# A transformer layer on one Trainium2 core: stores of the mixing part on SyncE's queue, w_o's sums on GpSimd behind markers, a second z, and GpSimd's arithmetic on VectorE

## The chip, the cores and the metric

The kernel runs on one core of one Trainium2 chip. The core has TensorE (PE in the profile; matmuls), VectorE (DVE), ScalarE (ACT), GpSimd (POOL) and SyncE (SP), which here does nothing but start DMA transfers. GpSimd starts DMAs as well: the two are the kernel's two DMA queues, and only GpSimd's can add to what is in DRAM. Each engine works off its own instructions in a fixed order; an instruction that waits holds up everything behind it on that engine, the start of a DMA too. The metric is the device time of one execution in microseconds (us); lower is better.

## The reference, cut to what matters

One layer over 512 tokens of width 2048, float32. The mixing part (attention with 8 heads of width 128, beside pooling) comes first, the feed-forward part after it:

```python
h = rms_norm(x, pre_mix_g)
z = h @ w_in                       # 2048 x 4096: [q | k | v | u], 1024 columns each
a = chunked_attention(q, k, v, rel_bias)   # 8 heads, chunks of 64 tokens
p = multiscale_pool(u, pool_w, pool_scale) # 4 groups, trailing means of 2, 4, 8, 16 tokens
x = x + rms_norm(concat(a, p) @ w_o, post_mix_g)
h = rms_norm(x, pre_ffn_g)
y = (gelu(dwconv3(h @ w_up)[:F]) * dwconv3(h @ w_up)[F:]) @ w_down
x = x + rms_norm(y, post_ffn_g)
```

In the pooling, a trailing mean is made from running sums (each doubling step adds a shifted copy), minus the token itself. In the attention, a mask puts −1e30 where a chunk would look ahead.

## The kernel before, in words

**Split products.** Each float32 operand is split into a rounded part and the rest: `split` (L136) has ScalarE write the rounded part (L138) and VectorE the rest (L139, or L142 with a scale). A product then takes three matmuls (`mm3`: L156, L158, L159), or a wide and a half one (`mm2`: L164, L170). A weight block is loaded by SP into a raw tile (`raw4`, five buffers), then split into `w4` tiles (names ending in h and l).

**Seven products for eight.** The large products are done by a scheme of seven block products, whose operands are sums of blocks of the weights and of x. Head 0's q and k are done plainly at the start, with x coming in. After that come the v stage for half of v (`v_steps(0)`), then the products for q and k of the other seven heads, pair by pair: `Pairs` loads four raw blocks ww, wx, wy, wz for each pair on SP (L444), `make` adds them on VectorE and splits each sum into wfh and wfl some four products ahead, `qk_product` does the matmuls and `qk_keep` gathers the seven results (za, zb, zm) into the tile z, 128 x 2 x 512, which holds q and −k of one head. There is one buffer for z. Each z is stored to DRAM, `zqk[h]`, by GpSimd (L567).

**The heads.** Then come heads 0 to 2, between the steps of the second half of v, and heads 3 to 7 between the eight blocks of u (`u0` to `u7`). `load_head` (L632) loads the head's bias and its zq on SP, multiplies zq by RR (the norm's factors) on GpSimd (L638), and splits it into qkh and qkl. `scores` does the score matmuls (s, L156 to L159) and the softmax on VectorE and ScalarE, with a memset of −1e30 on GpSimd for each of four blocks (L670); `turn` transposes the probabilities (pt, L688) and splits them into pth and ptl; `values` multiplies by v. The values of v wait in DRAM (`vd`, stored by `v_spill`, L393) and are loaded by `v_load` in two loads of 512 KB.

**Pooling.** `pool_keep` makes the running sums us from u with up to four additions on GpSimd (L710), and `pool_mix` multiplies by the group's matrix (pm). `spill_mix` writes the result to the single tile mx and stores it to `pooled` from GpSimd (L739).

**Work laid in between.** Two kinds of work prepare for later. *Ready blocks*: six parts of blocks of w_down are split early and stored as `rw..h` and `rw..l` (`keep_ready`, L275); `READY_AT` says at which v step. *Sums in DRAM*: `sums_in_dram` builds the sums of w_o's blocks (and of some of w_down's) in DRAM, wt and t, without the core's memory: a copy by SP (L306, not ahead of the last weight load), then additions by GpSimd (L309), step by step (`more_sums`). An addition waits for the copy under it.

A scheduler sets each engine's order from the code and from when tiles come free, and `issue_after` puts one instruction behind another, so the order shown below isn't the code's.

Of the kernel before, what the change touches and what calls it, by code (L numbers as in the profile page):

```python
# [9 lines left out]
F32 = mybir.dt.float32  # L10
F32R = mybir.dt.float32r
AF = mybir.ActivationFunctionType
ALU = mybir.AluOpType
# [32 lines left out]
def f32(ap):  # L46
    return ap.bitcast(F32)
# [32 lines left out]
def encoder_layer(ctx: ExitStack, tc: tile.TileContext, x, xT, vecs, rel, post_mix, post_ffn,  # L80
# [29 lines left out]
    def raw4(name):  # L110
        return big.tile([P, 1024], F32, tag="raw", bufs=5, name=name)
# [142 lines left out]
    READY = (0, 1), (1, 1), (0, 2)  # L254
    ready_w = {at: [dram.tile([P, CU, S], F32, name=f"rw{at[0]}{at[1]}{p}") for p in "hl"] for at in READY}

    READY_AT = {0: (7,), 1: (3, 4, 5, 6, 7)}
    ready_parts = [(at, j) for at in READY for j in range(2)]
    READY_OF = {0: ready_parts[:1], 1: ready_parts[1:]}

    def v_and_ready_specs(g):
        specs = []
# [7 lines left out]
    def keep_ready(g, n):  # L270
        if n not in READY_AT[g]:
            return
        (cc, i), j = READY_OF[g][READY_AT[g].index(n)]
        for dest, v in zip(ready_w[cc, i], weights.get(f"rw{cc}{i}_{j}")):
            nc.gpsimd.dma_start(dest[:, 2 * j:2 * j + 2, :], f32(v))  # L275

    specs = v_and_ready_specs(0)
    FIRST_PART = len(specs)
# [22 lines left out]

    def sums_in_dram():

        def copy(dest, source):
            with tc.issue_after(load_w.last):
                nc.sync.dma_start(dest, source)  # L306

        def add(dest, source):
            nc.gpsimd.dma_start(dest, source, accum_op=ALU.add)  # L309

        def wo_step(step, i, at):
            for cc in range(2):
                source = wo_block(cc, *at) if type(at) is tuple else wo_sum[at][cc]
                for k in range(2):
                    sl = slice(4 * k, 4 * k + 4)
                    step(wo_sum[i][cc][:, sl, :], source[:, sl, :])
                    yield

        for step, i, at in ((copy, 7, (1, 1)), (add, 7, (0, 1)), (copy, 5, (0, 0)), (add, 5, (0, 1)),
                            (copy, 6, 5), (add, 6, (1, 1)), (copy, 4, 6), (add, 4, (1, 0))):  # L320
            yield from wo_step(step, i, at)
# [46 lines left out]
    z0 = raw4("z0").rearrange("p (a b) -> p a b", a=2)  # L368
    nc.scalar.activation(z0[:, 0], ps0["q"], AF.Copy)
    nc.vector.tensor_scalar_mul(z0[:, 1], ps0["k"], -1.0)  # L370
    nc.gpsimd.dma_start(zqk[0], z0)

    def v_steps(i, ps):
        for n, c in enumerate(VORDER[i]):
# [13 lines left out]
    def v_spill(i, ps):  # L388
        for p in range(2):
            v = raw4(f"vs{p}").rearrange("p (a b) -> p a b", a=2)  # L390
            for t in range(2):
                nc.scalar.activation(v[:, t], ps[2 * p + t], AF.Copy)
            nc.gpsimd.dma_start(vd[i][:, 2 * p:2 * p + 2, :], v)  # L393

    def scaled(q):
        for kb in range(4 * q, 4 * q + 4):
# [32 lines left out]
    class Pairs:  # L429
# [12 lines left out]
        def load(self, k, i):  # L442
            def raw(what, tile_, m, kh):
                load_w.last = nc.sync.dma_start(tile_, w_qk[k + 1, m, kh]).ins  # L444
                self.raw[k, what] = tile_

            if i == 1:
                raw("x", p0.tile([P, 1024], F32, tag="wx", bufs=3, name="wx"), 0, 0)
                raw("w", raw4("ww"), 1, 0)
            elif i == 2:  # L450
                raw("z", p0.tile([P, 1024], F32, tag="wz", bufs=2, name="wz"), 0, 1)
            elif i == 5:
                raw("y", raw4("wy"), 1, 1)

# [58 lines left out]
    def more_sums(n):  # L513
        for _ in range(n):
            next(sums_step, None)

    BANK = {1: "a", 6: "a", 7: "a", 4: "a", 5: "g", 3: "g", 2: "d"}
    FIRST = 1, 5, 2
    TURNED = 6, 7, 4
# [21 lines left out]
    def qk_keep(k, i):  # L541
        if i == 1:
            qk_z[k, "1"] = qk_tile("za", 1, 2)
            nc.scalar.activation(whole_of(qk_z[k, "1"]), qk_banks[k, "a"], AF.Copy)
        elif i == 2:
            v = whole_of(qk_z[k, "1"])
            nc.vector.tensor_add(v, qk_banks.pop((k, "d")), v)
        elif i == 5:
            qk_z[k, "5"] = whole_of(qk_tile("zb", 1))
            nc.scalar.activation(qk_z[k, "5"], qk_banks[k, "g"], AF.Copy)  # L550
        elif i == 6:
            qk_z[k, "m"] = qk_tile("zm", 2)
            v = whole_of(qk_z[k, "m"][:, :1])
            nc.scalar.activation(v, qk_banks[k, "a"], AF.Copy)
            nc.vector.tensor_add(v, qk_banks.pop((k, "g")), v)
        elif i == 7:
            v = whole_of(qk_z[k, "m"][:, 1:])
            nc.scalar.activation(v, qk_banks[k, "a"], AF.Copy)
            nc.vector.tensor_add(v, qk_z.pop((k, "5")), v)
        elif i == 4:  # L560
            one, m, a = qk_z.pop((k, "1")), qk_z.pop((k, "m")), qk_banks.pop((k, "a"))
            z = p0.tile([P, 2, S], F32, tag="z", bufs=1, name="z")
            nc.vector.tensor_add(z[:, 0, :T], one[:, 0, 0], one[:, 0, 1])
            nc.vector.tensor_add(z[:, 1].rearrange("p (a b) -> p a b", a=2), m[:, :, 0], m[:, :, 1])
            nc.scalar.activation(z[:, 0, T:], a[:, T:], AF.Copy)
            nc.vector.tensor_add(z[:, 0, T:], a[:, :T], z[:, 0, T:])
            nc.gpsimd.dma_start(zqk[k + 1], z)  # L567

    def restore():
        for i in range(2):  # L570
            v = raw4(f"xr{i}").rearrange("p (a b) -> p a b", a=4)
            nc.sync.dma_start(v, xT[4 * i * P:4 * (i + 1) * P, T:].rearrange("(a p) n -> p a n", p=P))
            for a in range(4):
                split(*g_half(hT, 4 * i + a, 1), v[:, a, :], col(V_PREMIX, 4 * i + a))
# [27 lines left out]
    with tc.tile_pool(name="p1", bufs=2, reuse_waits="tile") as p1:  # L602
# [4 lines left out]
        for g, w in enumerate(WINDOWS):  # L607
            nc.gpsimd.memset(recip[:, g, :], 1.0 / w)
            for t in range(w - 1):
                nc.gpsimd.memset(recip[:, g, t:t + 1], 1.0 / (t + 1))  # L610

        pth = p1.tile([P, 1408], F32R, tag="pth", bufs=1, name="pth")
        ptl = p1.tile([P, 1408], F32R, tag="ptl", bufs=1, name="ptl")
        PT_AT, PT_Q = (0, 512, 896, 1152), (0, P, 2 * P, 2 * P)
# [18 lines left out]
        def load_head(h):  # L633
            state["bias", h] = t512("bias", bufs=1)
            nc.sync.dma_start(state["bias", h], rel[h])
            v = p1.tile([P, 2, S], F32, tag="zq", bufs=1, name="zq")
            nc.sync.dma_start(v, zqk[h])
            nc.gpsimd.tensor_mul(v, v, RR)  # L638
            pair = [p1.tile([P, 2, S], F32R, tag="qk" + p, bufs=1, name="qk" + p) for p in "hl"]
            split(*pair, v)  # L640
            state["qk", h] = [tuple(p[:, n, :] for p in pair) for n in range(2)]

        def v_load(i):
            vh, vl = (acc8(f"v{p}{i}", "B", F32R).rearrange("p (a b) -> p a b", a=NT) for p in "hl")
            for p in range(2):
                v = raw4(f"vr{p}").rearrange("p (a b) -> p a b", a=2)
                nc.sync.dma_start(v, vd[i][:, 2 * p:2 * p + 2, :])
                for n in range(2):
                    t = 2 * p + n
                    split(vh[:, t, :], vl[:, t, :], v[:, n, :], rt[:, t:t + 1])  # L650
            state["v"] = vh, vl

        def load_bias(h):
            state["bias", h] = t512("bias", bufs=1)
            nc.sync.dma_start(state["bias", h], rel[h])

        def scores(h):
            (q, k), bias = state.pop(("qk", h)), state.pop(("bias", h))
# [6 lines left out]
            for t in range(NT):  # L665
# [1 line left out]
                s = t512("s", bufs=4)  # L667
                nc.vector.scalar_tensor_tensor(s[:, :n], ps[:, :n], SCALE, bias[:, S - n:],
                                               op0=ALU.mult, op1=ALU.add)
                nc.gpsimd.memset(s[:CHUNK, n - CHUNK:n], -1e30)  # L670
                nm = p1.tile([P, 1], F32, tag="st", bufs=16, name="nm")
                nc.vector.tensor_reduce(nm, s[:, :n], axis=AX.X, op=ALU.max, negate=True)
                sm = p1.tile([P, 1], F32, tag="st", bufs=16, name="sm")
# [28 lines left out]
        def pool_keep(g, j, ps):  # L702
            w = WINDOWS[g]
            u = p1.tile([P, WIDE], F32, tag="u", bufs=1, name="u")[:, :PAD + S]
            nc.gpsimd.memset(u[:, :PAD], 0.0)
            nc.vector.tensor_mul(u[:, PAD:], ps, R)
            cur, step = u, 1
            while step < w:
                nxt = p1.tile([P, WIDE], F32, tag="us", bufs=2, name="us")[:, :PAD + S]
                nc.gpsimd.tensor_add(nxt[:, step:], cur[:, step:], cur[:, :PAD + S - step])  # L710
                if 2 * step < w:
                    nc.gpsimd.memset(nxt[:, :step], 0.0)
                cur, step = nxt, 2 * step
            edge = p1.tile([P, PAD], F32, tag="uf", bufs=2, name="uf")
            nc.vector.tensor_mul(edge, cur[:, PAD:2 * PAD], recip[:, g, :])
# [20 lines left out]
        def spill_mix(kb, ps, scale):  # L736
            v = t512("mx", bufs=1)
            nc.scalar.activation(v, ps, AF.Copy, scale=scale)
            nc.gpsimd.dma_start(pooled[:, kb - HEADS, :], v)  # L739

        def run(n):
            for _ in range(n):
# [27 lines left out]
        for j in range(8):  # L770
# [7 lines left out]
            if j < 7:  # L778
                pool_keep(j // 2, j % 2, ps)
                more_sums(2 if j == 6 else 1)  # L780
        u7 = ps
        mixT += [acc8(f"mixT{i}", "B").rearrange("p (a b) -> p a b", a=4) for i in (2, 3)]
        for n, sl in ((2, slice(0, 4)), (3, slice(0, 2))):
            nc.sync.dma_start(mixT[n][:, sl, :], pooled[:, 4 * (n - 2) + sl.start:4 * (n - 2) + sl.stop, :])
# [905 lines left out]
```

## Time and profile before

| what | us |
|---|---|
| median of 3 runs (lowest, highest) | 1959.24 (1959.15, 1963.5) |
| profiled execution | 1962.61 |
| its span | 1960.8 |
| TensorE busy in the span | 1865.3 (95%) |
| VectorE busy | 1530.2 (78%) |
| ScalarE busy | 1083.5 (55%) |
| GpSimd busy | 357.0 (18%) |

The change touches what runs in the first 500 us or so. By the profile's timeline the products for q and k run from about 81 us, the change-over to the heads and heads 0 to 2 end at about 348 us, and the u stage ends at about 487 us. A granted clock of 1.00 is TensorE's full clock. The profile's idle time stands beside the instruction that ended it and names what that one waited for. A DMA's landing is counted from its issue.

### The profile page before, as it was taken

The numbers are of one execution on the slowest core, as the hardware profiler recorded it, in microseconds if no ns is written. First come the engines' busy times: TensorE is split into PE (matmuls) and PEld (weight loads), VectorE is DVE, ScalarE is ACT, GpSimd is POOL, SyncE is SP. The second block draws the span as 40 slices with busy tenths as digits, with TensorE's granted clock in tenths as the row PEclk, the third lists the DMA queues.
The fourth block names the chain that finished last, engine by engine and source line by source line (L and its number), as shares of the span: only waits on it lengthen the run. The fifth ranks groups of instructions, "written<-read, shape, count | busy, mean of one in ns | idle before, by whom it ended". The sixth has DMA issues, their size and how long they took to land.

```text
span 1960.8 us, 25466 instructions
## 1 busy us (share of the span) xinstructions
PE 1865.3 (95%) x9598; PEld 1598.1 (81%) x9598; DVE 1530.2 (78%) x1704; ACT 1083.5 (55%) x1376; POOL 357.0 (18%) x446
## 2 busy tenths in 40 slices
PE   9977947979999999999999999999999999999998
PEld 7866836867788988888888888888888788888886
DVE  6956645764857898888888888888888889998886
ACT  7633424533654656565656665666665665565553
POOL 3311122233100002222122222222122000110111
PEclk9988968989999999999999999999999999999999
DMA  7589777788578659988888989898888977877785
GB/s 261 204 236 268 209 253 246 235 243 233 198 248 260 244 153 214 203 199 207 202 198 207 202 207 203 202 206 197 205 201 200 358 237 193 232 173 196 164 243 152
DMA packets 142747, 426.02 MB, mean 217 GB/s; under 512 B 12000, under 2 KB 15456, under 8 KB 137184
## 3 DMA queue, kind: packets, MB, share of 16 engines
q0 software_dynamic: 54320, 164.65, 42.8%
q1 hardware_dynamic: 88304, 259.75, 38.3%
q8 instruction: 75, 1.23, 0.2%
q14 instruction: 48, 0.39, 0.1%
HBM read 370.35 MB, written 104.33 MB: 242 GB/s over the span
## 4 chain that ended last, share of the span: by engine, by line
PE 79%; DMA 7%; DVE 6%; issue 3%; ACT 2%; POOL 2%; SPq 0%; DVEq 0%; POOLq 0%; ACTq 0%
PE qa L164 15%; PE qa L170 8%; PE qg L164 8%; PE qg L170 4%; PE qd L164 4%; PE pa L156 4%; PE pa L159 4%; PE pa L158 4%; PE m L158 2%; PE m L159 2%; PE m L156 2%; PE qd L170 2%; DMA zqk<-z 2%; PE pg L156 2%; PE pg L159 2%
## 5 line engine op out<-in xcount | busy, mean ns | idle before, releaser
L138 ACT ACTIVATE wfh<-wx 128x1024 fp32r<-128x1024 f32 x192 | 203.5, 1060 | 163.1 <-PE qg L164 52.1
L164 PE MATMUL qa<-gT,wfh 128*128 128x512 f32 x1152 | 290.3, 394 | 0.0
L139 DVE TENSOR_TENSOR wfl<-wx,wfh 128x1024 fp32r<-128x1024 f32 x192 | 234.5, 1221 | 51.0 <-ACT wfh L138 36.7
L164 PEld LDWEIGHTS qa<-gT,wfh 128*128 128x128 f32 x1152 | 208.7, 190 | 37.5
L1307 POOL DMA_DIRECT2D wx<-in_w_up x122 | 104.6, 857 | 500.8 <-DVE wfl L139 474.2
L170 PE MATMUL qa<-gT,wfl 128*128 128x256 f32 x1152 | 163.1, 285 | 9.8 <-DVE wfl L139 8.8
L170 PEld LDWEIGHTS qa<-gT,wfl 128*128 128x128 f32 x1152 | 153.0, 193 | 14.5 <-issue 9.0
L138 ACT ACTIVATE wfh<-wy 128x1024 fp32r<-128x1024 f32 x96 | 101.8, 1061 | 110.5 <-PE qg L164 59.8
L164 PE MATMUL qg<-h,wfh 128*128 128x512 f32 x656 | 162.2, 389 | 0.0
L164 PEld LDWEIGHTS qg<-h,wfh 128*128 128x128 f32 x656 | 122.9, 188 | 25.8 <-ACT zb L1363 0.5
L139 DVE TENSOR_TENSOR bl<-b,bh 128x2048 fp32r<-128x2048 f32 x56 | 127.2, 2286 | 19.3 <-ACT bh L138 11.7
L138 ACT ACTIVATE bh<-b 128x2048 fp32r<-128x2048 f32 x56 | 106.1, 1913 | 54.4 <-DVE b L1071 22.1
L156 PE MATMUL pa<-bh,ah 128*128 128x512 f32 x320 | 124.5, 389 | 0.0
L158 PE MATMUL pa<-bl,ah 128*128 128x512 f32 x320 | 124.5, 389 | 0.0
L159 PE MATMUL pa<-bh,al 128*128 128x512 f32 x320 | 124.5, 389 | 0.0
L139 DVE TENSOR_TENSOR wfl<-wy,wfh 128x1024 fp32r<-128x1024 f32 x96 | 117.1, 1219 | 7.6 <-ACT wfh L138 3.2
L139 DVE TENSOR_TENSOR wfl<-wz,wfh 128x1024 fp32r<-128x1024 f32 x48 | 58.7, 1223 | 56.7 <-PE qa L164 52.7
L164 PE MATMUL qd<-gT,wfh 128*128 128x512 f32 x384 | 95.0, 389 | 1.6 <-ACT wfh L138 1.6
L170 PEld LDWEIGHTS qg<-h,wfl 128*128 128x128 f32 x656 | 89.5, 190 | 6.4
L170 PE MATMUL qg<-h,wfl 128*128 128x256 f32 x656 | 91.5, 282 | 0.0
L164 PEld LDWEIGHTS qd<-gT,wfh 128*128 128x128 f32 x384 | 72.0, 188 | 16.8 <-ACT wfh L138 1.8
L1139 POOL DMA_DIRECT2D sum<-part x30 | 35.8, 1194 | 262.5 <-DVE part L1125 167.5
(561 smaller groups left out, 4475.8 us busy)
## 6 DMA issues: line engine op xcount, KB each, us to landing
wx<-in_w_up POOLq DMA_DIRECT2D x122, 512.0 KB, 6.3
b<-in_w_down SPq DMA_DIRECT2D x32, 1024.0 KB, 6.8
wx<-in_w_up SPq DMA_DIRECT2D x43, 512.0 KB, 5.3
wz<-in_w_up SPq DMA_DIRECT2D x41, 512.0 KB, 5.8
wy<-in_w_up SPq DMA_DIRECT2D x41, 512.0 KB, 4.7
wy<-in_w_up POOLq DMA_DIRECT2D x41, 512.0 KB, 6.6
sum<-part POOLq DMA_DIRECT2D x38, 512.0 KB, 7.1
wt<-in_w_o POOLq DMA_DIRECT2D x16, 1024.0 KB, 13.5
```

Source lines behind the costliest of these rows:

```text
L138: rounded = nc.scalar.activation(hi, src, AF.Copy)
L139: rest = nc.vector.tensor_sub(lo, src, f32(hi))
L156: nc.tensor.matmul(ps, l[0], r[0], start=first, stop=False, skip_group_check=onto)
L158: nc.tensor.matmul(low, l[0], r[1], start=False, stop=False, skip_group_check=onto)
L159: nc.tensor.matmul(ps, l[1], r[0], start=False, stop=last, skip_group_check=onto)
L164: nc.tensor.matmul(ps, w[0][:, kb], pairs[kb][0], start=fresh and not kb, stop=last, skip_group_check=not fresh)
L170: nc.tensor.matmul(ps[:, sl], w[1][:, kb], pair[:, sl], start=False, stop=last, skip_group_check=not fresh)
L1139: nc.gpsimd.dma_start(dest, v, accum_op=ALU.add)
L1307: nc.gpsimd.dma_start(self.raw[k, what], self.block(k, m, kh), accum_op=ALU.add)
```

## The change

1. *Stores through SP.* The stores of z (`zqk`, 8), v (`vd`, 4), the pooled blocks (6) and the ready blocks (12) are started by SP instead of GpSimd.
2. *Sums through GpSimd, with markers.* The copies of `sums_in_dram` are started by GpSimd too. Ahead of each copy or addition stands a marker: VectorE writes one column (`pace`, four buffers) behind a split, then GpSimd writes the same column, then GpSimd starts the DMA. It is off (`paced = False`) after u7.
3. *z in two buffers.* To make room, wz goes from its own two buffers to the five of `raw4`, and xr, two late loads of x, from there to those of wx.
4. *Arithmetic back to VectorE.* zq times RR, the running sums and their small memsets are VectorE's. The mask is written once for each head, into the bias (which is added to every block), in place of four times into the scores.
5. *Ready blocks.* Three parts are split in the first v stage (one before) and three in the second (five before).
6. *Places and v.* Tiles named "place" fix where u, us, bias, zq and qkh, qkl lie. `v_load` takes one load of 1 MB straight into vl and splits there.

```diff
-    READY_AT = {0: (7,), 1: (3, 4, 5, 6, 7)}
+    READY_AT = {0: (2, 4, 6), 1: (3, 5, 7)}
...
-            nc.gpsimd.dma_start(dest[:, 2 * j:2 * j + 2, :], f32(v))
+            nc.sync.dma_start(dest[:, 2 * j:2 * j + 2, :], f32(v))
...
+        def pace():
+            v = const.tile([P, 1], F32, tag="pace", bufs=4, name="pace")
+            with tc.issue_after(split.rest):
+                nc.vector.memset(v, 0.0)
+            return nc.gpsimd.memset(v, 1.0).ins
+
         def copy(dest, source):
+            if more_sums.paced:
+                with tc.issue_after(pace()):
+                    nc.gpsimd.dma_start(dest, source)
+                return
...
-            nc.gpsimd.dma_start(dest, source, accum_op=ALU.add)
+            with tc.issue_after(pace()) if more_sums.paced else nullcontext():
+                nc.gpsimd.dma_start(dest, source, accum_op=ALU.add)
...
-            nc.gpsimd.dma_start(vd[i][:, 2 * p:2 * p + 2, :], v)
+            nc.sync.dma_start(vd[i][:, 2 * p:2 * p + 2, :], v)
...
-                raw("z", p0.tile([P, 1024], F32, tag="wz", bufs=2, name="wz"), 0, 1)
+                raw("z", raw4("wz"), 0, 1)
...
-            z = p0.tile([P, 2, S], F32, tag="z", bufs=1, name="z")
+            z = p0.tile([P, 2, S], F32, tag="z", bufs=2, name="z")
...
-            nc.gpsimd.dma_start(zqk[k + 1], z)
+            nc.sync.dma_start(zqk[k + 1], z)
...
-            v = raw4(f"xr{i}").rearrange("p (a b) -> p a b", a=4)
+            v = p0.tile([P, 1024], F32, tag="wx", bufs=3, name=f"xr{i}").rearrange("p (a b) -> p a b", a=4)
...
+        for tag, bufs in (("u", 1), ("us", 2)):
+            p1.tile([P, WIDE], F32, tag=tag, bufs=bufs, name="place")
+        t512("bias", bufs=1)
+        for tag, dt in (("zq", F32), ("qkh", F32R), ("qkl", F32R)):
+            p1.tile([P, 2, S], dt, tag=tag, bufs=1, name="place")
...
             nc.sync.dma_start(state["bias", h], rel[h])
+            nc.vector.memset(state["bias", h][:CHUNK, S - CHUNK:], -1e30)
...
-            nc.gpsimd.tensor_mul(v, v, RR)
+            nc.vector.tensor_mul(v, v, RR)
...
-            for p in range(2):
-                v = raw4(f"vr{p}").rearrange("p (a b) -> p a b", a=2)
-                nc.sync.dma_start(v, vd[i][:, 2 * p:2 * p + 2, :])
-                for n in range(2):
-                    t = 2 * p + n
-                    split(vh[:, t, :], vl[:, t, :], v[:, n, :], rt[:, t:t + 1])
+            nc.sync.dma_start(f32(vl), vd[i])
+            for t in range(NT):
+                split(vh[:, t, :], vl[:, t, :], f32(vl)[:, t, :], rt[:, t:t + 1])
...
-                nc.gpsimd.memset(s[:CHUNK, n - CHUNK:n], -1e30)
...
-                nc.gpsimd.tensor_add(nxt[:, step:], cur[:, step:], cur[:, :PAD + S - step])
+                nc.vector.tensor_add(nxt[:, step:], cur[:, step:], cur[:, :PAD + S - step])
...
-            nc.gpsimd.dma_start(pooled[:, kb - HEADS, :], v)
+            nc.sync.dma_start(pooled[:, kb - HEADS, :], v)
...
+        more_sums.paced = False
```

How it moves instructions on the engines that wait. First GpSimd in the products for q and k, before: additions into w_o's sums (wt) and the stores of z in one line.

```order
L309 DMA wt_94<-in_w_o 128x4x512 x2
L309 DMA wt_95<-in_w_o 128x4x512
L567 DMA zqk_343<-z 128x1024
L309 DMA wt_95<-in_w_o 128x4x512
L567 DMA zqk_344<-z 128x1024
L309 DMA wt_96<-in_w_o 128x4x512 x2
L567 DMA zqk_345<-z 128x1024
L309 DMA wt_97<-in_w_o 128x4x512 x2
```

And GpSimd at the same place now (L313 are copies, L320 additions, into the same blocks):

```order
L308 MEMSET pace 128x1
L313 DMA wt_95<-in_w_o 128x4x512
L308 MEMSET pace 128x1
L313 DMA wt_95<-in_w_o 128x4x512
L308 MEMSET pace 128x1
L320 DMA wt_94<-in_w_o 128x4x512
L308 MEMSET pace 128x1
L320 DMA wt_94<-in_w_o 128x4x512
```

The stores have gone; each DMA has its marker ahead of it, and between a copy and the addition to it stand four markers.

SP in the same stage, before: the raw blocks of the pairs (L444) with the copies for w_o's sums (L306).

```order
L444 DMA ww<-in_w_qk 128x1024
L306 DMA wt_96<-in_w_o 128x4x512
L444 DMA wx<-in_w_qk 128x1024
L444 DMA wy<-in_w_qk 128x1024
L306 DMA wt_96<-in_w_o 128x4x512
L306 DMA wt_97<-in_w_o 128x4x512
```

And SP now, where the store of each z (L580) stands once among four blocks (L455):

```order
L455 DMA ww<-in_w_qk 128x1024
L580 DMA zqk_343<-z 128x1024
L455 DMA wz<-in_w_qk 128x1024
L455 DMA wx<-in_w_qk 128x1024
L455 DMA wy<-in_w_qk 128x1024
L455 DMA ww<-in_w_qk 128x1024
L580 DMA zqk_344<-z 128x1024
```

The copies have gone from this queue, and the blocks behind a store leave when the store has left.

VectorE in head 0, now, from the split of head 1's q and k on (L688 scales the softmax's blocks, L142 splits v, L654 masks the bias, L657 is zq times RR):

```order
L139 TENSOR_TENSOR qkl<-zq,qkh 128x1024
L307 MEMSET pace 128x1 x2
L139 TENSOR_TENSOR rw_0l<-rw_0r,rw_0h 128x1024
L142 SCALAR_TENSOR_TENSOR vl_2137<-vl_2137,rt,vh_2136 128x512 x4
L687 RECIPROCAL rs<-sm 128x1
L683 TENSOR_REDUCE nm<-s 128x1
L688 TENSOR_SCALAR s<-s,rs 128x256
L654 MEMSET bias 64x64
L657 TENSOR_TENSOR zq<-zq,RR 128x1024
L687 RECIPROCAL rs<-sm 128x1
L683 TENSOR_REDUCE nm<-s 128x1
L688 TENSOR_SCALAR s<-s,rs 128x384
```

In this piece of VectorE's order the splits of v, the mask and the product with RR stand between the softmax's blocks of head 0; before, the last two were GpSimd's.

More of the change, by code (lines that the diff above doesn't have):

```diff
@@ L255, in encoder_layer @@
     ready_w = {at: [dram.tile([P, CU, S], F32, name=f"rw{at[0]}{at[1]}{p}") for p in "hl"] for at in READY}
-    READY_AT = {0: (7,), 1: (3, 4, 5, 6, 7)}
+    READY_AT = {0: (2, 4, 6), 1: (3, 5, 7)}
     ready_parts = [(at, j) for at in READY for j in range(2)]
-    READY_OF = {0: ready_parts[:1], 1: ready_parts[1:]}
+    READY_OF = {0: ready_parts[:3], 1: ready_parts[3:]}
     def v_and_ready_specs(g):
@@ L370, in encoder_layer @@
     nc.vector.tensor_scalar_mul(z0[:, 1], ps0["k"], -1.0)
-    nc.gpsimd.dma_start(zqk[0], z0)
+    nc.sync.dma_start(zqk[0], z0)
     def v_steps(i, ps):
@@ L515, in more_sums @@
             next(sums_step, None)
+    more_sums.paced = True
     BANK = {1: "a", 6: "a", 7: "a", 4: "a", 5: "g", 3: "g", 2: "d"}
@@ L644, in v_load @@
             vh, vl = (acc8(f"v{p}{i}", "B", F32R).rearrange("p (a b) -> p a b", a=NT) for p in "hl")
-            for p in range(2):
-                v = raw4(f"vr{p}").rearrange("p (a b) -> p a b", a=2)
-                nc.sync.dma_start(v, vd[i][:, 2 * p:2 * p + 2, :])
-                for n in range(2):
-                    t = 2 * p + n
-                    split(vh[:, t, :], vl[:, t, :], v[:, n, :], rt[:, t:t + 1])
+            nc.sync.dma_start(f32(vl), vd[i])
+            for t in range(NT):
+                split(vh[:, t, :], vl[:, t, :], f32(vl)[:, t, :], rt[:, t:t + 1])
             state["v"] = vh, vl
-        def load_bias(h):
-            state["bias", h] = t512("bias", bufs=1)
-            nc.sync.dma_start(state["bias", h], rel[h])
         def scores(h):
@@ L704, in pool_keep @@
             u = p1.tile([P, WIDE], F32, tag="u", bufs=1, name="u")[:, :PAD + S]
-            nc.gpsimd.memset(u[:, :PAD], 0.0)
+            nc.vector.memset(u[:, :PAD], 0.0)
             nc.vector.tensor_mul(u[:, PAD:], ps, R)
@@ L709, in pool_keep @@
                 nxt = p1.tile([P, WIDE], F32, tag="us", bufs=2, name="us")[:, :PAD + S]
-                nc.gpsimd.tensor_add(nxt[:, step:], cur[:, step:], cur[:, :PAD + S - step])
+                nc.vector.tensor_add(nxt[:, step:], cur[:, step:], cur[:, :PAD + S - step])
                 if 2 * step < w:
-                    nc.gpsimd.memset(nxt[:, :step], 0.0)
+                    nc.vector.memset(nxt[:, :step], 0.0)
                 cur, step = nxt, 2 * step
```

## The prediction

> **What bounds the kernel now.** The page's head and its 40 slices (each digit the busy tenths of 49 us) come first.
>
> ```profile
> span 1960.8 us, 25466 instructions
> PE   9977947979999999999999999999999999999998
> ```
>
> TensorE is busy nearly everywhere but in the first third, which is where the change lies. The windows view sizes that: start and end, length, then busy time (and instructions) of PE, PEld, DVE, ACT, POOL, the granted clock, the DMA share, GB/s.
>
> ```profile
> 0.00:700.00 700.00, 614.57 (x3013) 519.03 (x3014) 471.89 (x615) 341.97 (x515) 135.56 (x190) 0.94 0.78 236
> 50.00:75.00 25.00, 25.00 (x116) 20.84 (x115) 23.76 (x18) 15.41 (x19) 10.67 (x7) 1.00 0.27 91
> 75.00:250.00 175.00, 149.85 (x816) 129.19 (x815) 110.35 (x119) 76.35 (x98) 19.47 (x20) 0.94 0.90 254
> 250.00:350.00 100.00, 59.74 (x261) 49.83 (x260) 55.25 (x97) 34.20 (x64) 26.95 (x64) 0.78 0.79 250
> 348.00:490.00 142.00, 128.49 (x613) 108.11 (x612) 87.30 (x169) 58.17 (x112) 45.90 (x71) 0.95 0.84 232
> ```
>
> TensorE idles 700 − 614.57 = 85.4 us here, of which 25.2 us in the query/key products (75 to 250), 40.3 us in the change-over to the heads and heads 0 to 2 (250 to 350), and 13.5 us in the u stage (348 to 490). The clock is below 1 in the same three stretches, so what is busy there is partly slow as well. No other engine is full: VectorE is busy 63%, 55% and 61% of them. So the waits decide, not the work. The waits view names them (engine and line waiting, what for, us in total, times, longest): first TensorE's, then one of VectorE's and two of GpSimd's.
>
> ```profile
> PE s L156 <- ACT qkh L138: 28.2, 1, 28.2
> PE pt L688 <- DVE s L677: 20.1, 4, 10.5
> PE qg L170 <- DVE wfl L139: 8.9, 1, 8.9
> PE qa L170 <- DVE wfl L139: 8.8, 1, 8.8
> PE qg L164 <- ACT zb L550: 4.8, 3, 2.5
> PE s L156 <- DVE ptl L139: 4.7, 1, 4.7
> PE m L158 <- DVE wo_0l L139: 3.6, 1, 3.6
> DVE z L563 <- DMA zqk<-z: 59.8, 6, 18.4
> POOL wt L309 <- DMA wt<-in_w_o: 63.7, 7, 14.5
> POOL wt L309 <- DMA wt<-wt: 46.3, 4, 21.5
> ```
>
> The timeline of the longest stall of the products shows how they hang together (start, length, engine and line; in brackets the idle time before and what ended it).
>
> ```profile
> 113.31 1.24 POOL L309 DMA_DIRECT2D wt<-in_w_o  x1 [13.38 <-DMA wt<-in_w_o]
> 114.05 1.07 POOL L567 DMA_DIRECT2D zqk<-z  x1
> 127.11 0.43 DVE L563 TENSOR_TENSOR z<-za 128x256 f32<-128x256 f32 x1 [18.35 <-DMA zqk<-z]
> 128.73 2.08 PE L170 MATMUL qg<-s,wfl 128*128 128x256 f32 x8 [8.92 <-DVE wfl L139]
> 172.63 1.09 PE L170 MATMUL qg<-s,wfl 128*128 128x256 f32 x8
> ```
>
> GpSimd stands 13.38 us at an add into w_o's sums until the copy under it has landed; the finished z waits behind it, its store leaves only at 114.05. There is one z, so VectorE waits for that store to land, until 127.11 (18.35 us), to write the next, and the weights' splits (wfl) stand behind that. TensorE runs dry 8.92 us, and its next eight matmuls take 2.08 us, where eight in an undisturbed place took 1.09.
>
> **The change, part by part.** *Query/key products (75 to 250).* With two z, VectorE needs the store of z two pairs back, and on SP that store stands behind no add. Both 8.9 us gaps go (17.7 us). Of the 4.8 us for zb, whose releaser is late by the same stall, and the remaining 2.7 us of the 25.2, I take 4 as gone. Each long gap costs about 1 us for each slow half product (2.08 − 1.09) and there are about two behind it: 2 x 2 = 4 us, of which I take 3. What it costs: the 44.5 MB moved in this stretch (254 GB/s x 175 us) must now move in about 150 us, 297 GB/s. The share of 0.90 would become 0.90 x 175 / 150 = 1.05, so loads can land late again. Every marker is also one small VectorE instruction. For these I put 6 us back, between 0 and 12 (the 12 being half of the gains again). Sum −19, between −10 and −26.
>
> The Trainium skill's page "DMA: Bandwidth & Descriptors", section "Issuing engines are not separate DMA queues", speaks against this item: DMAs from any engine run on the same 16 engines, and moving the start to another engine saves only the sequencer's time to start them, which is usually small. By it the item would bring about nothing; the two POOL rows with 13.38 us and 114.05 show a start that is late because of what stands ahead of it on the engine, not because of its own length, and there the page's "usually" doesn't hold.
>
> *Change-over and heads 0 to 2 (250 to 350).* The rows of the longest stall:
>
> ```profile
> 272.57 0.49 SPq L635 DMA_DIRECT2D bias<-in_rel  x1
> 273.11 0.78 SPq L637 DMA_DIRECT2D zq<-zqk  x1
> 281.07 2.33 POOL L638 TENSOR_TENSOR zq<-zq,RR 128x1024 f32<-128x1024 f32 x1 [6.01 <-DMA zq<-zqk]
> 284.55 0.58 PE L156 MATMUL s<-qkh 128*128 128x256 f32 x1 [28.24 <-ACT qkh L138]
> ```
>
> The load of head 0's z is issued only at 273.11, since the tiles it and the bias go to, and SP's rows ahead of them, come free late; then landing 8 us, GpSimd's product, the split, and s at 284.55. With the "place" tiles fixed in front, these loads wait only for an early product of the last pair. By the order they go out right behind the sixth pair's store, some 14 us after the last pair's second-last product, and TensorE wants s some 25 us after it. The 28.2 us go, and so do the 0.7 behind it and the 4.7 of head 1; the 6.7 us left of the 40.3 (before the transposes of head 1) stay.
>
> What is late next is in VectorE's order. In head 0 four splits of v stand ahead of the softmax's tail, and they wait for a 1 MB load into vl, which waits for SP and for vl's place; the bias's memset and the product for zq wait for their own loads there as well. These are the three DMA rows nearest to them (KB each, median us to landing; vr is half of what vl is) and the price of the product on either engine:
>
> ```profile
> zq<-zqk SPq DMA_DIRECT2D x8, 512.0 KB, 8.0
> vr<-vd SPq DMA_DIRECT2D x4, 512.0 KB, 8.6
> wt<-in_w_o POOLq DMA_DIRECT2D x16, 1024.0 KB, 13.5
> L638 POOL TENSOR_TENSOR zq<-zq,RR 128x1024 f32<-128x1024 f32 x8 | 20.1, 2510 | 25.9 <-DMA zq<-zqk 17.5 <-DVE s L677 8.4
> L139 DVE TENSOR_TENSOR qkl<-zq,qkh 128x1024 fp32r<-128x1024 f32 x8 | 9.7, 1217 | 0.0
> 290.44 2.39 POOL L638 TENSOR_TENSOR zq<-zq,RR 128x1024 f32<-128x1024 f32 x1
> 290.65 2.33 DVE L677 TENSOR_SCALAR s<-s,rs 128x256 f32<-128x256 f32 x1
> L706 DVE TENSOR_TENSOR u<-u,RR 128x512 f32<-128x512 f32 x8 | 5.5, 686 | 12.7 <-PE u L159 12.7
> ```
>
> The 1 MB load lies between 8.6 (512 KB) and 13.5 us; it leaves some 4 us before its splits' turn, so VectorE waits 5 to 10 us, then has 4 x 0.7 + 1.2 + 1.2 us of work ahead of the tail. I count 10 us of new gap at head 0 (5 to 13), and 2 at each of heads 1 and 2 beside the 6.7. Before, 28.2 + 0.7 + 4.7 = 33.6 went; so −33.6 + 14 = −20. The clock of 0.78 over these 100 us costs up to 0.22 x 59.7 = 13 us of matmul time; the gaps shrink from 40.3 to about 21, so a bit under half of it, 6 us, goes too. Of the five ready parts that stood here two move to the start; their splits, at 1.22 us on VectorE for each, were in its way: −2. Sum −28, between −15 and −38.
>
> *U stage (348 to 490).* The longest gap has this chain (ahead of it the store's KB and median landing):
>
> ```profile
> pooled<-mx POOLq DMA_DIRECT2D x6, 256.0 KB, 5.1
> 413.60 0.69 ACT L738 ACTIVATE mx<-pm,vec 128x512 f32<-128x512 f32 x1 [10.28 <-DMA pooled<-mx]
> 418.75 1.75 PE L688 MATMUL pt<-ident,s 128*128 128x128 f32 x7 [10.46 <-DVE s L677]
> ```
>
> ScalarE waits 10.28 us for the single mx, whose store stood on GpSimd among its adds; on SP it leaves at once, so 8 of the 10.46 go (the landing of 5.1 us stays, mostly covered). With the arithmetic off GpSimd the 3.6 us before the first w_o product go too, and 1.5 of slow clock: −13. Against it VectorE gets 20 adds at 0.68 us (13.6 us), six products of zq here at 1.22 (7.3) and small memsets (about 2): 23 us. GpSimd's arithmetic slows what VectorE does at the same time (290.65: 2.33 us, started 0.2 us behind GpSimd's 2.39); I count one such loss for each of the six products here, at 2.33 − 0.40, some 11 us. Net 12 on 87.3 busy of 142: still under 75%, so there is room, but part of it stands ahead of a tail. The second load of v costs a wait as the first did, some 5 us. I put 3 us back, between 0 and 10. Sum −10, between −3 and −18.
>
> *Start.* The v stage takes two more ready parts, 2 x 1.22 us on a VectorE that is busy 23.76 of 25 us (50 to 75): +2, between 0 and 4. Thirty issues moved from GpSimd to SP cost nothing by themselves: the two SP issues above took 0.49 and 0.78 us, and SP has waits in plenty. What matters is what stands behind them (below).
>
> Together −19 − 28 − 10 + 2 = −55, between −82 and −24. The profiled run took 1962.6 (1.8 beside its span), 3.4 above the median of the runs, 1959.2. I take 55 from 1959.2 and get 1904; the bounds are 1877 and 1935.
>
> **The rivals.** *VectorE becomes the pacer (chance 0.21).* Each head's product of zq and memset of the bias wait in VectorE's queue for loads ahead of the softmax's tail. If all eight heads pay 5 us more than the one stall that I count, 8 x 5 = 40 less the 17 that I have put in, the gain falls by 23: 1927; with a v-load at the upper end, 1935. For: 23.76 of 25 us. Against: 55 to 63% elsewhere.
>
> *The queue doesn't matter (chance 0.05).* If the stores land late because the DMA engines are full (share 0.90), another queue's start doesn't help: the z stall goes on through later loads, the 28.2 us turn into waits for the same bytes, and VectorE's extra work eats the rest. That is 1957, no change. It is what the page's rule above would give. Against it: 13.38 us of GpSimd standing at a copy with the store behind it.
>
> *VectorE gets GpSimd's waits through the markers (slower, chance 0.13).* A marker of VectorE waits for GpSimd's memset four markers back, and GpSimd's DMAs wait for copies (63.7 + 46.3 = 110 us in eleven waits before). By the order, some 24 markers go by in the 150 us of the products, one in 6 us, so VectorE has 4 x 6 = 24 us of slack. It decides from where a copy lands later than that: 13.5 us is the median landing, but 21.5 is the longest wait. With the DMA engines above their share, 24 adds and copies in eight groups that each land 9 us beyond the slack cost 8 x 9 = 72 us, all of it on the splits that TensorE waits for: 1904 + 72 = 1976. The loads behind the stores on SP act to the same side: there the slack is some 14 us of VectorE's work between a load and its split.
>
> **How the numbers follow.** The forecast (0.57) with its bounds, the first rival and 0.04 for a larger gain than the bounds (all of the 85 us) are faster: 0.82. No change, within 0.3% (6 us, about what a measurement of this kernel can tell): 0.05. Slower 0.13. The range goes to the end of the first rival and a little beyond both bounds, 1872 to 1946; what is left out is the third rival, the second, and little else.
>
> **What would show it.** In the profile after: VectorE's wait for zqk<-z near nothing; no gap over 3 us in the products, or else one that names wfl with a late load; s of head 0 ahead of 270 us; a gap of 5 to 13 us at the transposes of head 0, with VectorE idle before a split of v (vl); mx's wait below 5 us; VectorE's busy time up by 15 to 25 us in the u stage. I am wrong if VectorE's markers (pace) show waits of over 10 us in all, if SP's stores wait with loads behind them that TensorE then misses, or if the DMA share goes to 1 and the products' gaps stay.

## The result, and the profile after

The changed kernel takes 1925.85 us in the median (1924.27 to 1926.65) against 1960.24 before: a ratio of 0.9821, with a 95% interval of 0.9804 to 0.9838, or 34 us less. The forecast was 55 less. The page after, head and slices:

```profile
span 1924.1 us, 25433 instructions
PE   9999869999999999999999999999999999999998
```

The windows of after (columns as before), cut where its own stages end, and below them before's last two stages cut in the same way:

```profile
0.00:700.00 700.00, 658.34 (x3247) 556.24 (x3248) 524.22 (x758) 368.36 (x545) 86.89 (x149) 0.97 0.82 248
50.00:75.00 25.00, 23.93 (x111) 19.91 (x110) 24.96 (x19) 16.64 (x21) 7.87 (x4) 1.00 0.62 210
75.00:224.00 149.00, 145.54 (x814) 126.72 (x813) 114.32 (x143) 76.98 (x98) 20.83 (x67) 0.99 0.86 252
224.00:312.00 88.00, 61.34 (x256) 49.73 (x255) 49.97 (x104) 30.85 (x57) 7.88 (x16) 0.81 0.86 262
312.00:441.00 129.00, 124.69 (x607) 105.52 (x606) 90.86 (x218) 58.04 (x113) 13.51 (x25) 0.99 0.81 231
```

```profile
248.00:347.00 99.00, 58.74 (x255) 48.92 (x254) 52.82 (x93) 32.52 (x59) 26.43 (x63) 0.78 0.78 249
347.00:487.00 140.00, 126.63 (x609) 107.00 (x607) 84.73 (x166) 57.81 (x112) 45.90 (x71) 0.95 0.85 237
```

The products (75 to 224) now hold TensorE busy but for 3.5 us. The change-over with heads 0 to 2 (224 to 312) still idles 26.7 of 88 us, at a clock of 0.81. The waits of TensorE and VectorE name what is left:

```profile
PE pt L699 <- DVE s L688: 17.6, 6, 5.2
PE v L158 <- DVE v_6l L139: 6.4, 1, 6.4
PE s L156 <- DVE ptl L139: 3.9, 1, 3.9
PE qa L164 <- ACT vs L403: 3.5, 1, 3.5
DVE bias L654 <- DMA bias<-in_rel: 25.7, 5, 13.0
DVE zq L657 <- DMA zq<-zqk: 10.7, 3, 5.3
```

VectorE waits 36 us at two small jobs of its own, each head's mask and product, for loads that have not landed. The z wait (59.8 us before) is no longer among VectorE's waits. The timeline of the worst place:

```profile
209.32 0.38 SPq L653 DMA_DIRECT2D bias<-in_rel  x1
209.75 0.43 SPq L656 DMA_DIRECT2D zq<-zqk  x1
228.17 0.11 DVE L654 MEMSET bias<- 64x64 f32 x1 [12.98 <-DMA bias<-in_rel]
233.06 1.23 DVE L657 TENSOR_TENSOR zq<-zq,RR 128x1024 f32<-128x1024 f32 x1 [4.78 <-DMA zq<-zqk]
235.87 0.80 PE L158 MATMUL v<-v_6l,gT 128*128 128x512 f32 x1 [6.41 <-DVE v_6l L139]
```

Head 0's loads went out early, as forecast, but landed 18.8 and 23.3 us later; VectorE stood at a mask of 0.11 us, and the split v_6l stood behind.

One thing is seen only when the stages are laid side by side. The table gives each stage's length in us, between the starts of the first matmuls of each stage in the timelines: products; change-over and heads 0 to 2; u stage; w_o's products; and the rest (the feed-forward part, to the end of the span). The products are counted from the first matmul behind the transposes of R (`R<-ident`), which is the fourth product of the first pair: 84.1 us before, 87.1 after. The first three run ahead of it, from 73.4 and 74.6 us, so the products begin earlier than the 81 us given further up.

| kernel | products | heads 0–2 | u | w_o | rest |
|---|---|---|---|---|---|
| before | 163.9 | 99.4 | 139.6 | 165.2 | 1308.6 |
| after | 136.5 | 88.6 | 128.9 | 165.9 | 1317.1 |
| e1 tiles in their old place | 134.2 | 86.8 | 126.4 | 168.1 | 1304.5 |
| e2 before, tiles 128 bytes on | 165.0 | 96.6 | 137.2 | 164.8 | 1319.1 |
| e3 e1, four sums' DMAs later | 135.7 | 76.5 | 136.0 | 163.8 | 1304.0 |
| e4 e1, head 0's mask and product on GpSimd | 134.2 | 80.5 | 125.7 | 165.7 | 1305.7 |
| e5 e1, one z | 147.6 | 87.0 | 127.9 | 168.3 | 1303.9 |
| e6 e1, z stored by GpSimd | 135.7 | 83.0 | 129.1 | 165.8 | 1305.8 |
| e7 e1, no markers | 143.5 | 80.0 | 128.3 | 161.4 | 1306.5 |
| e8 e1, arithmetic on GpSimd | 135.7 | 83.5 | 127.7 | 172.2 | 1304.4 |
| e9 before, two z | 159.1 | 89.8 | 139.8 | 165.4 | 1304.2 |
| e10 e1, tiles 64 bytes on | 135.8 | 89.3 | 128.5 | 169.6 | 1313.0 |
| e11 e3 and e4 | 134.2 | 72.7 | 136.5 | 165.5 | 1304.5 |
| e12 e11, mask ahead of its load | 134.2 | 75.2 | 132.5 | 166.8 | 1305.2 |

From before to after, the part up to the feed-forward part (which starts at 652.2 and 607.0 us) is 45 us shorter. The rest, whose code the change doesn't touch, is 8.5 us longer, though TensorE's waits in it are shorter (0.3 us after, 2.6 before): 45.2 − 8.5 = 36.7, the difference of the two spans.

### The profile page after: what moved, and what is told of

It reads as the page before. It is cut to its first block, busy times and chain, and to the rows that moved or that the text cites. A ratio compares the mean times of both kernels' runs of the same rounds, so it can differ in the third digit from the quotient of the medians.

```text
span 1924.1 us, 25433 instructions
## 1 busy us (share of the span) xinstructions
PE 1873.8 (97%) x9598; PEld 1593.8 (83%) x9598; DVE 1541.6 (80%) x1800; ACT 1082.5 (56%) x1376; POOL 302.3 (16%) x398
## 4 chain that ended last, share of the span: by engine, by line
PE 86%; DVE 5%; DMA 5%; ACT 2%; issue 1%; SPq 0%; POOL 0%; DVEq 0%; POOLq 0%; ACTq 0%
PE qa L164 18%; PE qa L170 9%; PE qg L164 9%; PE qg L170 5%; PE qd L164 4%; PE pa L156 4%; PE pa L158 4%; PE pa L159 4%; PE qd L170 2%; PE m L158 2%; PE m L156 2%; PE m L159 2%; PE pg L156 2%; PE pg L158 2%; PE pg L159 2%; DMA zq<-zqk 1%
## 5 line engine op out<-in xcount | busy, mean ns | idle before, releaser
L164 PE MATMUL qg<-h,wfh 128*128 128x512 f32 x656 | 165.7, 394 | 0.0
L164 PE MATMUL qa<-h,wfh 128*128 128x512 f32 x328 | 83.2, 395 | 0.0
## 6 DMA issues: line engine op xcount, KB each, us to landing
wt<-in_w_o POOLq DMA_DIRECT2D x24, 1024.0 KB, 12.6
```

Of the source, the lines that this page charges most:

```text
L164: nc.tensor.matmul(ps, w[0][:, kb], pairs[kb][0], start=fresh and not kb, stop=last, skip_group_check=not fresh)
```

## The experiments

**e1 and e2: where the tiles lie.** The four marker columns take 32 bytes each in the first pool of the core's memory, and every tile allocated behind them moves by 128 bytes. A padding tile ("place", 224 bytes) stands in that pool. e1 takes the 128 bytes off it in the changed kernel; e2 adds them in the kernel before.

```diff
-    place(const, 224)
+    place(const, 96)      # e1, in the changed kernel; e2, in the kernel before: 352
```

> The changed kernel with one number altered: the padding tile at the front of the core's memory is 96 bytes in place of 224, so that the four marker columns (4 x 32 = 128 bytes) no longer push every tile behind them by 128 bytes; the large tiles lie where they lay before the change. In the profile after, the mixing part ended 45 us earlier than before, but the whole span is only 37 us shorter, and the feed-forward part's matmuls came 0.6% further apart with no idle time. Theory A (where the matmuls' operands lie sets their pace): the feed-forward part runs at its old pace, about 8.5 us less in all, some 1917 us, and groups of eight 128x512 matmuls there go back from 2.02 to 1.98 us. Rival B (the pace is a matter of the chip, or of TensorE having idled less in front): no difference, 1926.

> The kernel before with the padding tile at 352 in place of 224 bytes and nothing else: every tile behind it lies 128 bytes further on, as in the changed kernel. Theory A: the feed-forward part slows by 8 to 9 us, in all about 1968 us against 1960, with the mixing part as it was. Rival B: no difference.

e1: 1909.9 us, ratio to before 0.9742 (0.9727 to 0.9758). e2: 1972.1 us, ratio 1.0060 (1.0044 to 1.0077). Theory A holds, and costs more than I expected: e1 is 16 us below the changed kernel, 12.6 of the 16.4 us between the spans in the rest. In e2 the rest is 10.5 us longer than before's, the part ahead of it 4.7 us shorter. The group of 128x512 matmuls on h in the feed-forward part, in before, after, e1, e2 and e10 in that order (the last column but one is the mean of one in ns):

```profile
L164 PE MATMUL qg<-h,wfh 128*128 128x512 f32 x656 | 162.2, 389 | 0.0
L164 PE MATMUL qg<-h,wfh 128*128 128x512 f32 x640 | 161.7, 394 | 0.0
L164 PE MATMUL qg<-h,wfh 128*128 128x512 f32 x632 | 156.2, 389 | 0.0
L164 PE MATMUL qg<-h,wfh 128*128 128x512 f32 x656 | 165.7, 394 | 0.0
L164 PE MATMUL qg<-h,wfh 128*128 128x512 f32 x640 | 162.3, 394 | 0.0
```

389 ns where the tiles lie as in the kernel before, 394 where they lie 64 or 128 bytes on, whichever kernel it is. Not every group moves as much: the largest, `qa<-gT,wfh`, stays at 392 to 393 ns in all five.

**e10: by 64 bytes.**

```diff
-    place(const, 96)
+    place(const, 160)
```

> e1 with the padding tile at 160 in place of 96 bytes: everything behind it lies 64 bytes further on. By theory A (where the operands lie sets the matmuls' pace) the part behind the mixing takes between e1's 1304.5 and the changed kernel's 1317 us: near 1317 if any step off the old place costs, near 1304 if a multiple of 64 is enough.

1919.1 us, ratio 0.9797 (0.9770 to 0.9823), the rest 1313.0 (in an execution of 1925.8, the slowest of four): 64 bytes cost 9 of the 16 us in all and 8.5 of the 12.6 in the rest. How large a step must be to be free again was not tried, nor which of the tiles it is.

**e5, e6 and e9: is it the second z or the store's queue?**

```diff
-  z = p0.tile([P, 2, S], F32, tag="z", bufs=2, name="z")    # e5: bufs=1
...
-  nc.sync.dma_start(zqk[k + 1], z)                          # e6: nc.gpsimd
```

> e1 with one z again in place of two; the stores of z still go through SP. Theory G (it is the place of the store, not the second z, that ended the 8.9 us gaps): the store leaves when z is ready and lands in about 8 us, VectorE waits some 5 us for each pair, and the splits made four products (11 us) ahead cover that: the products (from 87.8 to 222.0 us in e1) get at most 3 us longer. Rival H (the second z is needed): VectorE's waits come through to TensorE again, 2 to 6 us for each of six pairs, 12 to 30 us longer.

> e1 with the seven stores of z in the products back on GpSimd's queue, between the marked copies and additions; z still has two buffers. By G (the place of the store decides) the stores leave up to 12 us late behind markers, but with two z a store has a whole pair's time (19.6 us) to land, so that here both theories expect little: within 3 us of e1 for the products, and up to 5 us more at the change-over, where the last stores are read back. If the products lengthen by over 10 us, GpSimd's queue is held by more than its markers.

> The kernel before with only the second z and what makes room for it (wz in the shared raw buffers, xr with wx); the stores stay on GpSimd behind unmarked additions, and the arithmetic stays there too. e5 and e6 say that the second z matters and the store's queue little once there are two. Theory P (the second z by itself carries the gain in the products): they shorten by 20 to 30 us, to about 135 to 145 us from 163.9, and the change-over keeps most of its 28 us gap; 1935 to 1945 in all. Rival Q (with GpSimd standing at copies for up to 21 us, two z are not enough, it takes the queue as well): the products shorten by at most 12 us, 1950 or more.

e5: 1921.5 us (0.9793; 0.9766 to 0.9821), products 147.6: 13.4 longer than e1, at the low end of rival H. e6: 1907.2 us (0.9710; 0.9677 to 0.9744), products 135.7, as expected. e9: 1946.0 us (0.9925; 0.9900 to 0.9951), in theory P's range, but by another way: the products only went to 159.1, which is rival Q's, and most of the rest came off the change-over, where the 28.2 us wait at s is down to 1.9. VectorE's wait for z in e5, then in e9 VectorE's, GpSimd's and TensorE's waits, and one place in its GpSimd:

```profile
DVE z L576 <- DMA zqk<-z: 43.2, 6, 10.2
```

```profile
DVE z L563 <- DMA zqk<-z: 22.9, 3, 8.6
POOL wt L309 <- DMA wt<-in_w_o: 76.0, 8, 24.0
PE qg L164 <- ACT zb L550: 15.4, 3, 6.1
PE s L156 <- ACT qkh L138: 1.9, 1, 1.9
144.82 1.24 POOL L309 DMA_DIRECT2D wt<-in_w_o  x1 [21.12 <-DMA wt<-in_w_o]
145.56 1.07 POOL L567 DMA_DIRECT2D zqk<-z  x1
```

So no part does it alone: of the 29.7 us between before's products and e1's, all but the second z brings 16.3 (e5), the second z with unmarked sums ahead of its store 4.8 (e9), all but SP's queue 28.2 (e6), and, looking ahead to e7, all but the markers 20.4. What z needs beside a second buffer is a store that stands behind no waiting addition; markers on GpSimd give that as well as SP's queue does: in e6's products none of GpSimd's waits names a copy. One z with its store on GpSimd behind markers was not run, and e9 lacks the other parts of the change too. My theory G was wrong in one step: the splits made ahead did not cover waits of 7 us for each pair.

**e7: no markers.**

```diff
-    more_sums.paced = True
+    more_sums.paced = False
```

> e1 without markers: additions go out on GpSimd as soon as their copies have landed, copies on SP behind the weight loads, as before the change (the tiles lie as in e1). Theory L (the markers only space out the traffic; the gain came from the stores' place and z): within 4 us of e1 in all. Rival M (unspaced sums fill the DMA engines and hold up weights and stores): the products get gaps of several us again, 8 to 25 us more than e1.

1906.1 us (0.9716; 0.9689 to 0.9742): 3.8 below e1, inside theory L's 4. But the stages move: products 9.3 longer, as rival M has it, then head 0 waits, and heads 0 to 2 and the w_o products are 7 us shorter each. GpSimd's wait at the copies, and TensorE's at head 0:

```profile
POOL wt L320 <- DMA wt<-in_w_o: 104.6, 8, 32.7
257.54 0.58 PE L156 MATMUL s<-qkh 128*128 128x256 f32 x1 [18.21 <-ACT qkh L138]
```

What the stages gain and lose nearly cancels: the two spans are 1907.7 and 1907.2 us.

**e8: the arithmetic.**

```diff
-            nc.vector.tensor_mul(v, v, RR)
+            nc.gpsimd.tensor_mul(v, v, RR)
...
-                nc.vector.tensor_add(nxt[:, step:], cur[:, step:], cur[:, :PAD + S - step])
+                nc.gpsimd.tensor_add(nxt[:, step:], cur[:, step:], cur[:, :PAD + S - step])
```

> e1 with the product of zq with RR for all heads and the running sums of the pooling (with their small memsets) back on GpSimd; the mask stays on VectorE and in the bias. Theory N (moving this arithmetic to VectorE took GpSimd's slowness and the sharing with it off the path, as the prediction's sum has it): 3 to 15 us more than e1, mostly in the u stage, and VectorE's operations that run beside GpSimd's products again take about 2.3 us in place of 0.4. Rival O (VectorE's load and its waits for zq are the dearer): 3 to 12 us less than e1, as with head 0 alone.

1914.8 us (0.9760; 0.9736 to 0.9783), 5 more than e1 (the intervals of the two ratios overlap): theory N's sign, not its place. The u stage is hardly longer (127.7 against 126.4) and heads 0 to 2 are 3 us shorter; 4 us come in the w_o products. There VectorE waits for one of GpSimd's last running sums, a split of w_o's weights (wo_2l) stands behind that in its order, and TensorE waits for the split:

```profile
DVE uf L726 <- POOL us L721: 7.3, 2, 6.9
444.05 0.79 PE L158 MATMUL m<-wo_2l,a 128*128 128x512 f32 x1 [3.81 <-DVE wo_2l L139]
```

In all TensorE waits 8.3 us in this stage and in e1 6.4, none of it at wo_2l, so this is a part of the 4 us and not the whole. The groups of e8 (product on GpSimd; a softmax scaling on VectorE) and the latter in the changed kernel:

```profile
L657 POOL TENSOR_TENSOR zq<-zq,RR 128x1024 f32<-128x1024 f32 x8 | 21.4, 2674 | 68.8 <-DMA zq<-zqk 59.9 <-ACT s L685 9.0
L688 DVE TENSOR_SCALAR s<-s,rs 128x512 f32<-128x512 f32 x8 | 7.6, 947 | 0.1
L688 DVE TENSOR_SCALAR s<-s,rs 128x512 f32<-128x512 f32 x8 | 3.9, 483 | 0.1
```

VectorE's scaling of the widest block falls from 947 to 483 ns in the mean when GpSimd does not compute beside it; the three narrower blocks take the same in both (409 and 407 ns for 128x384). And GpSimd waits 59.9 us for zq's loads in e8, without heads 0 to 2 getting longer.

**e3, e4, e11 and e12: the wait at head 0.**

```diff
 # e3: no step at the last four places of the products, two in place of one at u0 to u3
-        if i in (3, 7, 4) and (k, i) != (0, 3):
+        if i in (3, 7, 4) and (k, i) != (0, 3) and k < pairs.n - 1 and (k, i) != (pairs.n - 2, 4):
             more_sums(1)
 # e4
-            nc.vector.memset(state["bias", h][:CHUNK, S - CHUNK:], -1e30)
+            (nc.vector if h else nc.gpsimd).memset(state["bias", h][:CHUNK, S - CHUNK:], -1e30)
...
-            nc.vector.tensor_mul(v, v, RR)
+            (nc.vector if h else nc.gpsimd).tensor_mul(v, v, RR)
 # e12: the mask first, then the bias in two loads that leave its corner out
+            b = state["bias", h]
+            nc.vector.memset(b[:CHUNK, S - CHUNK:], -1e30)
+            nc.sync.dma_start(b[:CHUNK, :S - CHUNK], rel[h][:CHUNK, :S - CHUNK])
+            nc.sync.dma_start(b[CHUNK:], rel[h][CHUNK:])
```

> e1 with four of the DMAs for w_o's sums (the DRAM-to-DRAM copies of 1 MB that go out with their markers at 209, 212, 240 and 243 us in the profile after) put off to the u stage, where four steps make two in place of one; all else in the same order. In the profile after, head 0's bias takes 18.8 us and its zq 23.3 us to land, and VectorE stands 13.0 and 4.8 us at the bias's mask and at zq's product, with the split v_6l behind them (TensorE's 6.4 us gap). Theory C (these loads are late because the DMA engines are full at that time): the loads land some 8 us earlier, the 6.4 and 2.5 us gaps shrink to under 4 together, 3 to 8 us less than e1 in all. Rival D (the loads wait for something else, or what fills the engines are the loads themselves): the landings stay over 15 us and the time within 2 us of e1.

> e1 with two instructions moved: the mask of head 0's bias and head 0's product of zq with RR are on GpSimd, so VectorE no longer waits for these loads ahead of v_6l. Theory E (the order on VectorE turns late loads into a gap): the 6.4 us gap at v_6l goes, s of head 0 then waits at most 2 to 4 us more than in the profile after, 4 to 8 us less than e1 in all. Rival F (TensorE only gets as far as s and waits there for the same load): the gap moves to s, and the time stays within 2 us of e1.

> e3 and e4 together: four sums' DMAs put off to the u stage, and head 0's mask and product on GpSimd. e3 took 3.7 and e4 9.4 us off the mixing part of e1 (603.2). If both shorten the wait for the same loads, they do not add up: 590 to 594 for the mixing part, about 1900 in all; if they add up, 590, 1896.

> e11 with the mask written ahead of the bias's load, which goes in two parts around the masked corner: VectorE's mask then waits for no transfer. By theory E (an instruction that waits for a transfer in VectorE's order holds up the softmax's tail) the waits at the mask (25.7 us in five in the profile after) go, and 2 to 8 us come off the heads beside e11. Rival: the product of zq stands right behind it and waits for a load as late, so at most 2 us come off.

e3: 1906.8 us (0.9725; 0.9709 to 0.9742). e4: 1904.2 us (0.9710; 0.9690 to 0.9731). e11: 1903.0 us (0.9714; 0.9689 to 0.9739). e12: 1903.3 us (0.9705; 0.9679 to 0.9730). The mask's wait in e1 and in e3:

```profile
227.28 0.11 DVE L654 MEMSET bias<- 64x64 f32 x1 [13.71 <-DMA bias<-in_rel]
```

```profile
224.52 0.11 DVE L654 MEMSET bias<- 64x64 f32 x1 [9.75 <-DMA bias<-in_rel]
```

With four DMAs fewer the loads take some 4 to 6 us less to land (zq 16.3 in place of 22.0 us), the gap at v_6l goes, 4.6 us are left of the two gaps, and heads 0 to 2 are 10 us shorter: theory C, at about half its size. But the u stage, where the four now lie, is 10 us longer; what e3 keeps comes off the w_o products. In e4, GpSimd waits for the same late loads and VectorE does not:

```profile
230.91 2.33 POOL L657 TENSOR_TENSOR zq<-zq,RR 128x1024 f32<-128x1024 f32 x1 [3.27 <-DMA zq<-zqk]
234.39 0.58 PE L156 MATMUL s<-qkh 128*128 128x256 f32 x1 [4.14 <-ACT qkh L138]
```

The 5.18 us gap that e1 has at v_6l is gone, 4.14 stay at s, and heads 0 to 2 are 6.3 us shorter: theory E. e11 nearly adds the two in heads 0 to 2 (72.7: 14.1 of 16.6 us) and loses 10 us in the u stage as e3 did; its part ahead of the feed-forward, 596.2 us, lies above both forecasts. In e12, where VectorE writes head 0's mask too, the waits change their name only. VectorE's in e11, then e12:

```profile
DVE bias L654 <- DMA bias<-in_rel: 17.0, 4, 8.2
```

```profile
DVE zq L659 <- DMA zq<-zqk: 16.7, 5, 6.1
```

The rival held. e4, e11 and e12 can't be told apart; any of them, at about 1903 to 1904 us, beats both kernels, by 2.9% and 1.2%. e3, e6 and e7 have medians of 1906 to 1907, and their runs overlap with those of these three.

## Why the prediction came out as it did

- **The sign, and the mechanism in the products: right, under-sized.** The 8.9 us gaps were the wait for z. I took 19 us and it was 27.4 (163.9 to 136.5): 23.5 us of gaps, all that these products had; the other 4 go with the clock, 0.99 in place of 0.94. The step that failed is the 6 us put back for full DMA engines: the share stayed at 0.86 (75 to 224), and no gap in the products names a late weight. By e5, e6, e7 and e9 it took both the second z and a store that stands behind no waiting addition.
- **The Trainium skill's rule** ("DMA: Bandwidth & Descriptors", "Issuing engines are not separate DMA queues"), by which the issuing engine matters little: e6 agrees with it (135.7 and 134.2 us), e7 beside e9 does not (two z and no markers in both: 143.5 us with the store on SP, 159.1 on GpSimd, though e9 lacks the other parts of the change). As far as these runs show, it holds where the queue doesn't stand at another transfer.
- **The change-over: right in the longest wait, over-sized in all.** The 28.2 us went, but the place tiles that I gave as the reason are not needed for it: in e9, which has none, head 0's zq leaves at 231.2 us in place of 273.1, and 1.9 us of the wait are left. What the places do by themselves was not run. I took the load of zq at 8.0 us from its median; it took 23.3. The cost of full DMA engines that I had put into the products came out here, on loads issued behind the weights of the next stage; e3 shows a part of it. Nor was VectorE's new wait at the load of v, where I had put it (that landed in 6.3 us), but at the masks and zq's products: 27.6 us from 224 to 312. TensorE's new gaps were 26.2 us (6.4, 2.5, 4.5, 5.2, 2.5, 1.2 and 3.9) against the 21 in the sum. The 6 us of clock did not come back either: without the gaps, the same matmuls took 59.1 us before (99.4 − 40.3), 62.4 after (88.6 − 26.2) and 59.6 in e1 (86.8 − 27.2). Forecast −28, measured −10.8.
- **The u stage: the sum right, its parts less so.** Forecast −10, measured −10.7; the 10.5 us gap went, 3.8 came, and the longest wait at mx fell from 10.3 to 5.7 us. VectorE's busy time rose by 6 us, not by the 12 of the sum or the 15 to 25 named as a sign: less work came over than I had counted, 16 additions (11.1 us) and three products of zq (3.6) in this stage in place of 20 and six. Of what GpSimd's arithmetic had slowed, some 9 us went, against the 11 in the sum.
- **The start: the size about right, half of it in another place.** The first product of the pairs starts 1.1 us later. The products counted in the table start 3.0 us later, since v's eviction waits for a raw buffer that wz now shares (3.5 us in the waits above, 4.3 in e9, which shares it too).
- **Left out altogether: where the tiles lie.** 8.5 us in the rest of the profiled run; e1 puts the whole of it at 16 us. Without this term the forecast of 1904 stands against 1910 in e1, and that closeness is in part luck: in the changed kernel the products gave 8 us more than forecast, the change-over 17 less.
- **The rivals.** The first (VectorE as the pacer) names a wait that is there: 36 us at masks and products; but its 1927 is close to the result by chance: 16 us of it are the tiles' place, and taking head 0's two waits off VectorE (e4) gains only 6. The markers did not pass GpSimd's waits on: no row has VectorE waiting for one.

## What to carry to other kernels

Two changes that each look sufficient for one stall can need one another: a second buffer gives a store time, and what stands ahead of the store in its queue decides whether it starts in that time; try each alone. A small instruction that waits for a load, put on an engine whose order feeds the critical one, hands the load's delay on, so price it at the landing in a full stage, not at the median. After an edit to a first pool, look at the stages that were not edited: if they run at another pace, check where the tiles lie before reading the result.

## What the runs showed of the hardware

I had not expected that a shift of all large tiles by 64 or 128 bytes changes the pace of matmuls: 128x512 ones on h go from 389 to 394 ns in the trace. The rest, some 1305 us, gets 8.5 us (e10 against e1), 10.5 (e2 against before) and 12.6 (after against e1) longer, in both kernels and with at most 2.6 us of TensorE's waits in it. These runs do not show which tile or which address matters.
